# Attention scores of two heads on the two halves of the TensorE array, three products each

## The chip, the core and the metric

The kernel runs on one core of a Trainium2 chip. TensorE (PE in the profile) multiplies matrices: it loads a stationary operand of up to 128 rows and 128 columns (a weight load, PEld) and streams a moving operand through it into a bank of PSUM. VectorE (DVE), ScalarE (ACT) and GpSimd (POOL) do the elementwise work, SyncE (SP) issues the DMAs. The engines work through their own queues in order and wait for each other by semaphores. The metric is the device time of one execution in microseconds, the median of several runs.

## The reference

One layer of an encoder block on 1024 tokens of width 2048. A normalised input is projected to 5632 columns. Half of the heads do windowed softmax attention, the others a bidirectional retention; both branches are normalised and gated, mixed by an output projection, added to the input and normalised again. What matters here is the attention: 16 query heads of 64 values share 4 key/value heads, and a block of 128 queries sees its own block of keys and the two beside it.

```python
qb = q.reshape(B, nb, BLOCK, ATTN_KV_HEADS, ATTN_GROUP, ATTN_HEAD_DIM)
...
s = jnp.einsum('bnqhgd,bnkhd->bhgnqk', qb, kb).astype(jnp.float32) * scale
...
s = jnp.where(valid[None, None, None], s + bias[None], -1e30)
...
m = jnp.maximum(jnp.max(s, axis=-1, keepdims=True), sink_b)
p = jnp.exp(s - m)
p = p / (jnp.sum(p, axis=-1, keepdims=True) + jnp.exp(sink_b - m))
out = jnp.einsum('bhgnqk,bnkhd->bnqhgd', p.astype(v.dtype), vb)
```

So a pair of heads over one block of queries needs two score matrices of 128 queries by 384 keys (256 at the two ends of the sequence), with 64 terms in each sum.

## The kernel before, in words

**Precision.** Large products are made in float32r. A float32 operand is split (`split`, L103) into a high part, rounded to float32r by a copy on ACT (L104), and a low part, the difference, by a subtraction on another engine through the helper `tt` (recorded at L98). A product is then three products: high by high, high by low, low by high.

**Main products.** The input projection is a loop over 22 units of 256 columns; each unit goes through 16 slices of the contraction (k), and in each slice over four output banks (tag M) with three products a bank (L808 to L810, or L801 to L803 for units laid out token by token). Weights come in by SP's DMAs, two tiles ahead. The output projection (L890 to L892, L917 to L919) follows with the same pattern.

**Work beside them.** Attention and retention are Python generators. After each bank's products, `point()` counts one point and, if `pace` points have gone by, lets the first generator in `jobs` run to its next `yield` (`pump`). That is how one step of attention comes to stand between main products in TensorE's queue. `pace` is 4.5, 4.5, 3 and 3.8 points for the four attention groups. Nothing else sets the order of TensorE's work; the framework may move an independent instruction of another engine a little ahead in that engine's own queue.

**One attention job** (`attn_job`) is one key/value head with its four query heads. The keys are loaded twice, into rows 0 to 63 and again into rows 64 to 127, and split into `kh` and `kl`. The four query heads are two pairs (`pr`), the sequence is eight blocks (`n`); `b` counts the 16 pairs of head pair and block. Step `t` handles one head (`c`, 0 or 1) of pair `b`, so that there are 32 steps and some to finish. In step `t`:

- the scores of head `c` go into one of two score banks (`pS`, tag S): two products, L434 and L435, each of 128 rows. The rows of the query tile `q[:, c, :]` hold the high part of the 64 query values in one half and the low part in the other, and the keys stand in both halves, so that one product gives (high + low) by `kh`, the other (high + low) by `kl`: four partial products in two;
- DVE adds the bias, takes the maximum and writes the result to a tile P (L441), ACT takes the exponential (L445), and in the odd step the two heads' sums are finished and P is scaled (L453);
- in even steps from 6 on, the values of an earlier pair are multiplied (L465, L466);
- four steps after its scores, P is transposed by TensorE into the bank T (`pT`, of which there is one; L493) and split into PTh (ACT, L504) and PTl (DVE, L98).

`q_parts` makes the query tile for two blocks of a head pair: for each head a copy of 64 rows on ACT (L420) and a subtraction of 64 rows on DVE; one of the two crosses to the other half of the rows.

The prediction also uses two places outside attention: the retention's scores (`s_t`, L563, products of 64 rows) and state products (`kv`, L578, 128 rows), each written as four products and shown in the trace as eight instructions, and the column sums of `attn_norm` (L514), made on rows 0 to 63 and then on rows 64 to 127.

Of the kernel before, what the change touches and what calls it, by code (L numbers as in the profile page):

```python
# [9 lines left out]
F32 = mybir.dt.float32  # L10
F32R = mybir.dt.float32r
AF = mybir.ActivationFunctionType
ALU = mybir.AluOpType
# [19 lines left out]
def hybrid_block(ctx: ExitStack, tc: tile.TileContext, a: dict, out: bass.AP):  # L33
# [54 lines left out]
    def pS():  # L88
        return psum("S", 2)
# [7 lines left out]
    def tt(eng, o, x, y, op):  # L97
        eng.tensor_tensor(o, x, y, op)  # L98
# [29 lines left out]
                )  # L128
            A.copy(dst[:, 512 * h : 512 * h + 512], p)

# [1 line left out]
    wraw, wsp, wide = {}, {}, [None]  # L132

    def w_src(i):
# [19 lines left out]
            split(hi, lo, r, G if i < W_IN_TILES else V)  # L154
            wsp[i] = (hi, lo)

# [1 line left out]
    jobs, aux = deque(), deque()  # L158
    step = [0]
    done = set()  # L160
# [35 lines left out]
            except StopIteration:  # L196
                queue.popleft()

# [1 line left out]
    xraw = {}  # L200

    def x_load(k):
# [28 lines left out]
        yield  # L231

    def bias_rows():
        # rows of relative bias with the window's mask, repeated for the skewed read
        oh = t2()
        SP.dma_start(oh[0:33, :], a["onehot"])
        ra = small(16, "ra")
        G.memset(ra[32:33, :], 1.0)
        SP.dma_start(ra[0:32, :], a["rel_bias"])
        yield  # L240
        p = pS()
        T.matmul(p[:16, :], ra[0:33, :], oh[0:33, :], start=True, stop=True)
        bt = t2()
        V.tensor_copy(bt[:16, :], p[:16, :])
        b16 = bt[:16, :]
        SP.dma_start(bd, b16.unsqueeze(1).to_broadcast([16, 128, 512]))
        done.add("bias")
        yield
# [28 lines left out]
    def decay():  # L277
        dc = small(24, "dc")
        for dst0, name in ((0, "ret_decay_fwd"), (8, "ret_decay_bwd")):
            s = a[name]  # L280
            SP.dma_start(dc[:, dst0 : dst0 + 8], bass.AP(tensor=s.tensor, offset=s.offset, ap=[[0, 128], [1, 8]]))
            q = 16 + dst0 // 2
            for par in range(2):
                SP.dma_start(
                    dc[64 * par : 64 * par + 64, q : q + 4],
                    bass.AP(tensor=s.tensor, offset=s.offset + par, ap=[[0, 64], [2, 4]]),
                )
        jc = small(2, "jc")
        SP.dma_start(jc, a["jcol"])
        yield  # L290
        # log sigmoid: min(d, 0) - log1p(exp(-|d|)), log1p(u) = 2 atanh(u / (2 + u))
        u, z, z2, acc, lg = (small(24, n) for n in ("lu", "lz", "lz2", "lacc", "lg"))
        V.tensor_scalar(z, dc, -1.0, None, ALU.mult)
        tt(V, z, z, dc, ALU.min)
        A.activation(u, z, AF.Exp)
        V.tensor_scalar(z, u, 2.0, None, ALU.add)
        V.reciprocal(z, z)
        tt(V, z, z, u, ALU.mult)
        tt(V, z2, z, z, ALU.mult)
        yield  # L300
        V.tensor_scalar(acc, z2, 2.0 / 17, 2.0 / 15, ALU.mult, ALU.add)
        for k in (13, 11, 9, 7, 5, 3, 1):
            tt(V, acc, acc, z2, ALU.mult)
            V.tensor_scalar(acc, acc, 2.0 / k, None, ALU.add)
        tt(V, acc, acc, z, ALU.mult)
        V.tensor_scalar(lg, dc, 0.0, None, ALU.min)
        tt(V, lg, lg, acc, ALU.subtract)
        yield
        A.activation(cdec, lg[:, :16], AF.Exp, scale=128.0)
        V.tensor_scalar(kdec[:, 0:8], lg[:, 0:8], jc[:, 0:1], None, ALU.mult)  # L310
        V.tensor_scalar(kdec[:, 8:16], lg[:, 8:16], jc[:, 1:2], None, ALU.mult)
        A.activation(kdec, kdec, AF.Exp)
        V.tensor_scalar(kdec, kdec, 0.125, None, ALU.mult)
        yield
        ab = t2()
        SP.dma_start(ab, a["masks"])
        yield
        yield
        for h in range(8):
            o = t2() if h % 4 == 0 else o  # L320
            oo = o[:, 128 * (h % 4) : 128 * (h % 4) + 128]
            V.tensor_scalar(oo, ab[:, 0:128], lg[:, h : h + 1], None, ALU.mult)
            stt(V, oo, ab[:, 128:256], lg[:, 8 + h : 9 + h], oo, ALU.mult, ALU.add)
            A.activation(oo, oo, AF.Exp)
            V.tensor_scalar(oo, oo, 0.125, None, ALU.mult)
            SP.dma_start(dd[h], oo)
            yield
        for p in range(4):
            o = t2() if p % 2 == 0 else o
            oo = o[:, 256 * (p % 2) : 256 * (p % 2) + 256]  # L330
            A.activation(oo[:, 0:128], ab[:, 256:384], AF.Exp, scale=lg[:, 16 + p : 17 + p])
            A.activation(oo[:, 128:256], ab[:, 384:512], AF.Exp, scale=lg[:, 20 + p : 21 + p])
            SP.dma_start(qdd[p], oo.rearrange("p (d i) -> p d i", d=2))
            yield
        done.add("decay")

# [1 line left out]
    def k_post(tiles):  # L338
        while "rb" not in done:
            yield  # L340
# [7 lines left out]
    def gate_post(tiles, et0, key, late=None):  # L348
        for b, g in tiles:
            et, hf = b // 2, b % 2  # L350
            # 2 silu(g) = g (1 + tanh(g / 2)); the half is in ew
            e = t2()
            A.activation(e, g, AF.Tanh, scale=0.5)
            yield
            stt(V, g, e, 1.0, g, ALU.add, ALU.mult)
            c = et0 + et
            if late is None:
                SP.dma_start(gd[128 * c : 128 * c + 128, 512 * hf : 512 * hf + 512], g)
            else:
                yield  # L360
                while ("ret", 3) not in done:
                    yield
                late(et, hf, g)
            yield
        done.add(key)
# [15 lines left out]
                yield  # L381
        done.add(("rope", p))

# [1 line left out]
    acc = [None]  # L385

    def attn_job(g, q_tiles, start):
# [26 lines left out]
        def q_parts(b2):  # L414
            pr, n = divmod(2 * b2, 8)
            q = att.tile([128, 2, 256], F32R, tag="qj", name=nm("qj"), bufs=2)
            src = q_tiles[pr][:, 128 * n : 128 * n + 256]
            for c in range(2):
                s0, s1 = 64 * c, 64 * (1 - c)
                A.copy(q[s0 : s0 + 64, c, :], src[s0 : s0 + 64, :])  # L420
                tt(V, q[s1 : s1 + 64, c, :], src[s0 : s0 + 64, :], q[s0 : s0 + 64, c, :].bitcast(F32), ALU.subtract)
            qj[b2] = q

        q_parts(0)
        for t in range(32 + 8):
            if t < 32:
                b, c = divmod(t, 2)
                pr, n = divmod(b, 8)
                head = 4 * g + 2 * pr + c
                m0, m1 = max(n - 1, 0), min(n + 2, 8)  # L430
                W, k0 = 128 * (m1 - m0), 128 * (m0 - n + 1)
                q = qj[b // 2][:, c, 128 * (n % 2) : 128 * (n % 2) + 128]
                p = pS()
                T.matmul(p[:, :W], q, kh[:, 128 * m0 : 128 * m1], start=True, stop=False)  # L434
                T.matmul(p[:, :W], q, kl[:, 128 * m0 : 128 * m1], start=False, stop=True)  # L435
                if c == 0:
                    st[b] = tuple(small(2, w, 4) for w in ("nmx", "sums", "esk"))
                nmx, sums, esk = st[b]
                x = att.tile([128, 384], F32, tag="P", name=nm("P"), bufs=5)
                P[t] = x  # L440
                V.tensor_tensor_reduce(  # L441
                    x[:, :W], p[:, :W], bias[2 * pr + c][:, k0 : k0 + W], -1.0, nsink[:, head : head + 1],
                    ALU.add, ALU.min, nmx[:, c : c + 1],
                )
                A.activation(x[:, :W], x[:, :W], AF.Exp, bias=nmx[:, c : c + 1], scale=-1.0, accum_out=sums[:, c : c + 1])  # L445
                if c == 1:
                    tt(V, esk, nmx, sink[:, head - 1 : head + 1], ALU.add)
                    A.activation(esk, esk, AF.Exp)
                    tt(V, sums, sums, esk, ALU.add)
                    V.reciprocal(sums, sums)  # L450
                    for cc in range(2):
                        y = P[t - 1 + cc]
                        V.tensor_scalar(y[:, :W], y[:, :W], sums[:, cc : cc + 1], None, ALU.mult)  # L453
                if t in (4, 16):
                    load_bias(2 if t == 4 else 3)
                if t % 4 == 2 and t + 2 < 32:
                    q_parts(t // 4 + 1)
# [73 lines left out]
        done.add("attn_norm")  # L531
        yield

# [1 line left out]
    retp = [None]  # L535

    def ret_job(p, rq, rk, vt, start):
# [159 lines left out]
        yield  # L697
        done.add(("ret", p))

# [1 line left out]
    rbA = {}  # L701

    def mixed_row(pool, kk, hf, gate=None):
# [10 lines left out]
            stt(V, r, r, ew[:, kk : kk + 1], gate, ALU.mult, ALU.mult)  # L714
        split(hi, lo, r)

# [1 line left out]
    def evac(u, b, p, st):  # L718
        kind, i = UNITS[u]
        hf = b % 2  # L720
# [56 lines left out]
    for u, (kind, i) in enumerate(UNITS):  # L777
# [3 lines left out]
        for k in range(NK):  # L781
# [48 lines left out]
                mixed_row(retp[0], k - 1, 0)  # L830
            if kk == 1:
                del wsp[wi]
        # what follows from the unit
        if u == 1:
            drain(aux, "k")
        if kind == "ka":
# [236 lines left out]
```

## Time and profile before

| | |
|---|---|
| time, median of 3 runs | 1603.08 us (1602.11 to 1606.64) |
| span of the profiled execution, first to last instruction | 1599.8 us |
| TensorE busy in the span | 1539.1 us (96%) |
| weight loads busy | 1327.7 us (83%) |
| DVE, ACT, POOL busy | 800.2, 524.7, 414.2 us |
| mean granted TensorE clock | 0.987 |

The page gives no time for the profiled execution beyond its span. A busy time adds up the durations of instructions where they don't overlap; a matmul's own duration runs from its start to the end of its last result, and consecutive matmuls overlap, so what one costs the next is read from the distance of their starts. A group's row ends with the engine's idle time just before the group and what ended it.

### The profile page before, as it was taken

The page shows a single profiled execution, that of the slowest core. Times are in us where ns is not written, and L with a number is a line of the kernel's source. Part 1 is how long each engine was busy: PE and PEld are TensorE (multiplying, and loading weights), DVE is VectorE, ACT ScalarE, POOL GpSimd, SP SyncE. Part 2 cuts the span into 40 slices and gives each one's busy share as a digit, 9 for nine tenths or more (in the row PEclk, how much of TensorE's full clock was granted, in tenths as well). Part 3 has the DMA queues.
Part 4 walks back from the last instruction along what each step waited for, and adds up shares of the span by engine and source line. Part 5 has one row for each costly group of instructions (what it writes and reads, how often), then busy time and mean ns, then how long its engine had stood idle before and what let it go on. Part 6 is the DMA issues. An engine that isn't in the chain of part 4 may idle for free.

```text
span 1599.8 us, 22578 instructions
## 1 busy us (share of the span) xinstructions
PE 1539.1 (96%) x8338; PEld 1327.7 (83%) x8338; DVE 800.2 (50%) x1888; ACT 524.7 (33%) x1186; POOL 414.2 (26%) x435
## 2 busy tenths in 40 slices
PE   8947999999999999999999999999999999999997
PEld 6936888888888887888898898998998888888886
DVE  5520126662576368567624734825747563473323
ACT  5311125552455356445511111111122343433210
POOL 2201222333344334424332332323322000220000
PEclk9978999999999999999999999999999999999999
DMA  8785311331123213212231221311322465574423
GB/s 298 252 100 131 96 53 45 91 106 56 49 84 108 58 44 111 64 51 80 57 102 55 82 80 47 99 60 50 103 80 93 159 223 158 172 245 149 122 63 112
DMA packets 108442, 167.52 MB, mean 105 GB/s; under 512 B 17419, under 2 KB 38923, under 8 KB 108204
## 3 DMA queue, kind: packets, MB, share of 16 engines
q1 hardware_dynamic: 108332, 166.09, 34.9%
q8 instruction: 65, 1.06, 0.3%
q14 instruction: 45, 0.37, 0.1%
HBM read 134.06 MB, written 31.98 MB: 104 GB/s over the span
## 4 chain that ended last, share of the span: by engine, by line
PE 81%; DVE 8%; DMA 4%; issue 3%; ACT 2%; POOL 1%; SPq 0%; POOLq 0%; ACTq 0%; DVEq 0%
PE psM L808 14%; PE psM L810 13%; PE psM L809 13%; PE psM L891 4%; PE psM L890 4%; PE psM L892 4%; PE psM L802 3%; PE psM L803 3%; PE psM L801 3%; DMA wr<-in_w_in 3%; PE psT L493 2%; DVE t L101 2%; PE psS L891 1%; PE psS L890 1%; PE psS L892 1%
## 5 line engine op out<-in xcount | busy, mean ns | idle before, releaser
L808 PE MATMUL psM<-hT,wh 128*128 128x512 f32 x1088 | 442.0, 406 | 6.3 <-DVE hT L220 6.3
L810 PE MATMUL psM<-hT,wl 128*128 128x512 f32 x1088 | 425.9, 392 | 2.0 <-POOL wl L98 2.0
L809 PE MATMUL psM<-hT,wh 128*128 128x512 f32 x1088 | 425.2, 391 | 0.0
L98 POOL TENSOR_TENSOR wl<-wr,wh 128x512 fp32r<-128x512 f32 x176 | 234.2, 1331 | 602.2 <-ACT wh L104 590.5
L104 ACT CAST wh<-wr 128x512 fp32r<-128x512 f32 x288 | 178.5, 620 | 605.7 <-PE psM L809 225.6
L810 PEld LDWEIGHTS psM<-hT,wl 128*128 128x128 f32 x1088 | 204.7, 188 | 47.5 <-POOL wl L98 2.5
L808 PEld LDWEIGHTS psM<-hT,wh 128*128 128x128 f32 x1088 | 205.2, 189 | 44.4 <-issue 6.2
L809 PEld LDWEIGHTS psM<-hT,wh 128*128 128x128 f32 x1088 | 205.6, 189 | 37.3 <-DVE hT L101 0.7
L801 PE MATMUL psM<-wh,hT 128*128 128x256 f32 x640 | 184.0, 288 | 31.2 <-ACT wh L104 31.2
L802 PE MATMUL psM<-wl,hT 128*128 128x256 f32 x640 | 182.6, 285 | 2.3 <-POOL wl L98 2.3
L803 PE MATMUL psM<-wh,hT 128*128 128x256 f32 x640 | 182.2, 285 | 0.0
L801 PEld LDWEIGHTS psM<-wh,hT 128*128 128x128 f32 x640 | 124.0, 194 | 32.4 <-ACT wh L104 31.4
L98 DVE TENSOR_TENSOR wl<-wr,wh 128x512 fp32r<-128x512 f32 x112 | 84.6, 756 | 131.7 <-ACT wh L104 131.5
L802 PEld LDWEIGHTS psM<-wl,hT 128*128 128x128 f32 x640 | 124.0, 194 | 3.1 <-POOL wl L98 3.0
L803 PEld LDWEIGHTS psM<-wh,hT 128*128 128x128 f32 x640 | 123.9, 194 | 0.0
L441 DVE CUSTOM_DVE_ANT_0 P<-psS,bias,nsink 128x384 f32<-128x384 f32 (+1 forms) x128 | 74.2, 580 | 90.6 <-PE psS L435 90.2
L445 ACT ACTIVATE P<-P,nmx 128x384 f32<-128x384 f32 (+1 forms) x128 | 75.6, 590 | 94.6 <-DVE nmx L441 93.2
L890 PE MATMUL psM<-wh,hT 128*128 128x512 f32 x256 | 100.0, 390 | 0.0
L891 PE MATMUL psM<-wl,hT 128*128 128x512 f32 x256 | 99.7, 390 | 0.0
L892 PE MATMUL psM<-wh,hT 128*128 128x512 f32 x256 | 99.6, 389 | 0.0
L98 DVE TENSOR_TENSOR t<-psM,rb 128x512 f32<-128x512 f32 x64 | 42.2, 684 | 106.4 <-PE psM L810 64.9
L98 POOL TENSOR_TENSOR acc<-acc,sq 64x128 f32<-64x128 f32 x112 | 55.1, 492 | 155.8 <-ACT sq L474 145.8
(200 smaller groups left out, 2261.6 us busy)
## 6 DMA issues: line engine op xcount, KB each, us to landing
wr<-in_w_in SPq DMA_DIRECT2D x176, 256.0 KB, 2.7
wr<-in_w_out SPq DMA_DIRECT2D x112, 256.0 KB, 2.7
t<-in_x SPq DMA_DIRECT2D x16, 512.0 KB, 6.0
mr<-md SPq DMA_DIRECT2D x32, 256.0 KB, 2.9
xr<-in_x SPq DMA_DIRECT2D x32, 256.0 KB, 3.9
out<-y SPq DMA_DIRECT2D x32, 256.0 KB, 2.8
t<-in_xT SPq DMA_DIRECT2D x15, 512.0 KB, 5.1
gd<-t SPq DMA_DIRECT2D x28, 256.0 KB, 2.3
```

The costliest lines, as they stand in the source:

```text
L98: eng.tensor_tensor(o, x, y, op)
L104: A.copy(o_hi, x)
L445: A.activation(x[:, :W], x[:, :W], AF.Exp, bias=nmx[:, c : c + 1], scale=-1.0, accum_out=sums[:, c : c + 1])
L801: T.matmul(po, hh[:, sl], wh[:, ws], start=first and z == 0, stop=False, skip_group_check=True)
L802: T.matmul(po, hh[:, sl], wl[:, ws], start=False, stop=False, skip_group_check=True)
L803: T.matmul(po, hl[:, sl], wh[:, ws], start=False, stop=last, skip_group_check=True)
L808: T.matmul(p, wh[:, ws], hh[:, sl], start=first, stop=False)
L809: T.matmul(p, wh[:, ws], hl[:, sl], start=False, stop=False)
L810: T.matmul(p, wl[:, ws], hh[:, sl], start=False, stop=last)
L890: T.matmul(p, mh, wh, start=(k == 0), stop=False)
L891: T.matmul(p, mh, wl, start=False, stop=False)
L892: T.matmul(p, ml, wh, start=False, stop=(k == NK - 1))
```

## The change

`q_parts` splits both heads in place: the tile's first half-plane holds the high parts of both heads (head 0 on rows 0 to 63, head 1 on rows 64 to 127), the second their low parts, with one copy and one subtraction of 128 rows. A new function `score_pair` makes the scores of both heads of a pair in the even step, in two banks taken at once. Each head's products use only its own 64 rows of the query tile and of the keys, and there are three: high by `kh`, low by `kh`, high by `kl` (the product of the two low parts is no longer made). They are issued alternately for head 0 and head 1. The odd step issues no score products and takes the bank made before. The rest of each step is as it was; other lines of the diff only remove comments.

```diff
         def q_parts(b2):
             pr, n = divmod(2 * b2, 8)
             q = att.tile([128, 2, 256], F32R, tag="qj", name=nm("qj"), bufs=2)
-            src = q_tiles[pr][:, 128 * n : 128 * n + 256]
-            for c in range(2):
-                s0, s1 = 64 * c, 64 * (1 - c)
-                A.copy(q[s0 : s0 + 64, c, :], src[s0 : s0 + 64, :])
-                tt(V, q[s1 : s1 + 64, c, :], src[s0 : s0 + 64, :], q[s0 : s0 + 64, c, :].bitcast(F32), ALU.subtract)
+            split(q[:, 0, :], q[:, 1, :], q_tiles[pr][:, 128 * n : 128 * n + 256])
             qj[b2] = q
+
+        scores = {}
+
+        def score_pair(b):
+
+            n = b % 8
+            m0, m1 = max(n - 1, 0), min(n + 2, 8)
+            W, keys = 128 * (m1 - m0), slice(128 * m0, 128 * m1)
+            qs = slice(128 * (n % 2), 128 * (n % 2) + 128)
+            ps2 = (pS(), pS())
+            for part, kx in ((0, kh), (1, kh), (0, kl)):
+                for c in range(2):
+                    r = slice(64 * c, 64 * c + 64)
+                    T.matmul(
+                        ps2[c][:, :W], qj[b // 2][r, part, qs], kx[r, keys],
+                        start=kx is kh and part == 0, stop=kx is kl,
+                    )
+            scores[b] = ps2
...
-                q = qj[b // 2][:, c, 128 * (n % 2) : 128 * (n % 2) + 128]
-                p = pS()
-                T.matmul(p[:, :W], q, kh[:, 128 * m0 : 128 * m1], start=True, stop=False)
-                T.matmul(p[:, :W], q, kl[:, 128 * m0 : 128 * m1], start=False, stop=True)
+                if c == 0:
+                    score_pair(b)
+                p = scores[b][c]
```

## The prediction

> **What bounds the kernel now.** I began with the page's head, its busy shares and the shares of the chain that ended last.
>
> ```profile
> span 1599.8 us, 22578 instructions
> PE 1539.1 (96%) x8338; PEld 1327.7 (83%) x8338; DVE 800.2 (50%) x1888; ACT 524.7 (33%) x1186; POOL 414.2 (26%) x435
> PE 81%; DVE 8%; DMA 4%; issue 3%; ACT 2%; POOL 1%; SPq 0%; POOLq 0%; ACTq 0%; DVEq 0%
> ```
>
> TensorE sets the time: it is busy for 96% of the span and holds 81% of the chain. The change touches only the attention jobs, so I then asked for the forms of the score products (L434 and L435), whose first and last starts in the trace are at 231 and 793 us, for the busy times from 231 to 800 us, and for all that PE waited for there.
>
> ```profile
> L434 PE MATMUL psS<-t,qj 128*128 128x384 f32 x96 | 32.5, 339 | 0.0
> L435 PE MATMUL psS<-t,qj 128*128 128x384 f32 x96 | 32.3, 336 | 0.0
> L435 PE MATMUL psS<-t,qj 128*128 128x256 f32 x32 | 9.0, 281 | 0.0
> L434 PE MATMUL psS<-t,qj 128*128 128x256 f32 x32 | 9.0, 281 | 0.0
> ...
> 231.00:800.00 569.00, 562.74 (x2883) 477.71 (x2882) 343.80 (x900) 281.34 (x741) 206.72 (x258) 1.00 0.24 72
> ...
> PE psT L493 <- DVE PTl L98: 3.8, 8, 1.2
> PE psO L466 <- DVE PTl L98: 1.9, 4, 1.0
> ```
>
> The third row gives PE, PEld, DVE, ACT, POOL, then the granted clock (1.00). PE is busy 562.74 of 569.00 us while DVE has 343.80 and ACT 281.34. PE's waits there come to 3.8 + 1.9 = 5.7 us, all for the low halves of the transposed probabilities, none for a score bank (psS). So whatever TensorE needs more or less for the scores goes almost whole into the end. There are 96/2 = 48 pairs of heads with 384 keys and 32/2 = 16 with 256 at the edges of the sequence.
>
> Durations of matmuls overlap, so costs are read from starts. Columns of the following rows: start, duration, engine, line.
>
> ```profile
> 402.63 0.39 PE L810 MATMUL psM<-hT,wl 128*128 128x512 f32 x1
> 402.86 0.34 PE L434 MATMUL psS<-t,qj 128*128 128x384 f32 x1
> 403.03 0.34 PE L435 MATMUL psS<-t,qj 128*128 128x384 f32 x1
> 403.21 0.39 PE L808 MATMUL psM<-hT,wh 128*128 128x512 f32 x1
> ...
> 399.88 0.28 PE L434 MATMUL psS<-t,qj 128*128 128x256 f32 x1
> 400.00 0.28 PE L435 MATMUL psS<-t,qj 128*128 128x256 f32 x1
> 400.11 0.39 PE L808 MATMUL psM<-hT,wh 128*128 128x512 f32 x1
> ```
>
> A main product takes 402.86 - 402.63 = 0.23 us of the array, a score product 0.35 / 2 = 0.175 us with 384 keys and 0.23 / 2 = 0.115 us with 256, and nothing is lost between main products and scores.
>
> **The change, part by part.** *Score products.* Removed: four products of 128 rows a pair, 4 x 0.175 = 0.70 us, or 4 x 0.115 = 0.46 us at an edge; 48 x 0.70 + 16 x 0.46 = 41.0 us in all. Added: six products of 64 rows a pair (384 matmuls and weight loads instead of 256), alternately on the upper and the lower half of the array. If the halves work side by side, a pair takes three of them: 0.525 or 0.345 us, 48 x 0.525 + 16 x 0.345 = 30.7 us, a gain of 10.3 us. If they work one after the other it is six: 1.05 or 0.69 us, 61.4 us, a loss of 20.4 us. The trace has one place where 64-row work changes halves, the column sums of L514 (eight instructions on rows 0 to 63, then eight on rows 64 to 127), and one form with eight on one half, L563. Here are their weight loads, with the loss of array time ahead of the first in brackets.
>
> ```profile
> 820.81 1.44 PEld L514 LDWEIGHTS psS<-ones,acc 64*128 64x128 f32 x16
> ...
> 869.19 0.96 PEld L563 LDWEIGHTS psS<-t,t 64*128 64x128 f32 x8 [0.35 <-issue]
> ...
> L563 PEld LDWEIGHTS psS<-t,t x128: 182/188/188, 854.7 to 1231.9; 64*128 64x128 f32 x128
> ```
>
> One load lasts 0.188 us, so in a string on one half they follow each other every (0.96 - 0.19) / 7 = 0.11 us. Sixteen one after the other would need 15 x 0.11 + 0.19 = 1.84 us; L514's took 1.44. For about 0.4 us the two strings ran together, although they are issued string after string; the change issues them alternately. The row is of two-column products, so it shows loads and issue overlapping, not two streams of 384 keys. I take side by side and keep both ends. The second stream starts behind the first by something between 0 and one load, 0.11 us: 0 to 7.0 us over 64 pairs. I take 0.03 us, near the lower end since L514's loads overlapped, which is 1.9 us. *What a page says of that offset.* The Trainium skill, "TensorE: Matmul & The Clock Gate", section "Part 3: Packing small matmuls — row/col tiling", puts packed products on different tiles about 4 ns apart; by it the offset would be 64 x 0.004 = 0.3 us, an estimate, and the sum 1.6 us lower. No run here shows that figure so far.
>
> *Going to half the array and back.* Each pair now sits between 128-row work on both sides. The trace has the same thing with and without the half: the retention's state products (L578, 128 rows) and its scores (L563, 64 rows), both eight instructions between a main L810 and L808.
>
> ```profile
> 861.62 0.39 PE L810 MATMUL psM<-hT,wl 128*128 128x512 f32 x1
> 861.85 1.05 PE L578 MATMUL psS<-v,t 128*128 128x128 f32 x8
> 862.66 0.48 PE L808 MATMUL psM<-hT,wh 128*128 128x512 f32 x1
> 862.97 0.40 PE L809 MATMUL psM<-hT,wh 128*128 128x512 f32 x1
> ...
> 868.88 0.39 PE L810 MATMUL psM<-hT,wl 128*128 128x512 f32 x1
> 869.20 1.16 PE L563 MATMUL psS<-t,t 64*128 64x128 f32 x8
> 870.28 0.50 PE L808 MATMUL psM<-hT,wh 128*128 128x512 f32 x1
> 870.62 0.39 PE L809 MATMUL psM<-hT,wh 128*128 128x512 f32 x1
> ```
>
> From L810 to L809 it is 862.97 - 861.62 = 1.35 us with 128 rows and 870.62 - 868.88 = 1.74 us with 64: 0.39 us for the way in and out. It lies ahead of the first load (L563's bracket above): the next weights are not loaded while the last product still runs. Nothing covers it, as PE has no other work. 64 pairs x 0.39 = 25.0 us. This is the largest term; its ends are the same, as the stretch is seen with and without it.
>
> *The query split.* Removed: half of 64 copies on ACT and of 64 subtractions on DVE, each of 64 rows.
>
> ```profile
> L420 ACT CAST qj<-t x64: 389/404/408, 223.2 to 764.9; 64x256 fp32r<-64x256 f32 x64
> L98 DVE TENSOR_TENSOR qj<-t,qj x64: 418/421/1411, 223.9 to 765.8; 64x256 fp32r<-64x256 f32 x64
> ```
> ...
> L104 ACT CAST wh<-wr 128x512 fp32r<-128x512 f32 x288 | 178.5, 620 | 605.7 <-PE psM L809 225.6
> ...
> L98 DVE TENSOR_TENSOR t<-psM,rb 128x512 f32<-128x512 f32 x64 | 42.2, 684 | 106.4 <-PE psM L810 64.9
> ```
>
> The 128-row form with 256 columns isn't in the trace; it costs between the 64-row form (0.404 and 0.421 us) and the 128-row form with twice the columns (0.620 and 0.684). At the first, which has the same columns, ACT loses 32 x 0.404 = 12.9 us and DVE 32 x 0.421 = 13.5 us; at the second 6.0 and 5.1. All lies beside PE's work and can reach the end only through the 5.7 us that PE waits for DVE.
>
> *The order.* The second head's products move one step ahead: past the main products between two steps (three to four and a half points of three, 0.69 us each) and ahead of the even step's value products and transposes. No DMA moves. In the odd step the transposes lose 0.35 us of lead over DVE; in the even step DVE's first score pass comes about 0.4 us later (0.525 + 0.03 + the way in, 0.2, against 0.35), and all behind it as well; with no slack on DVE that would return as 64 x 0.4 = 26 us, but DVE is idle for 225 of the 569 us, and I take none of it. Both score banks must now be free in the even step, one of them a step after its last use instead of two.
>
> ```profile
> DVE P L441 <- PE psS L435: 90.2, 69, 3.2
> L441 DVE CUSTOM_DVE_ANT_0 P<-psS,bias,nsink x128: 470/612/619, 231.5 to 794.3; 128x384 f32<-128x384 f32 x96, 128x256 f32<-128x256 f32 x32
> ```
>
> In 69 of 128 steps DVE stood waiting for the scores, so it is seldom a step behind; a bank wait would cost at most one pass of 0.612 us a pair, 39 us, at least nothing, and I take nothing. For the 5.7 us of waits I take half as gone, because every pair gives DVE more time and four steps save it 0.42 us: -2.9 us. The ends are -5.7 and, if the odd steps' lost lead shows at each of these 12 waits, 12 x 0.35 = +4.2 us.
>
> **Sum**: 25.0 - 10.3 + 1.9 - 2.9 = +13.7 us on the profiled span of 1599.8, that is 1613.5. The median of the runs is 1603.08, 3.3 us over that span; with the same 3.3 around it the prediction is 1617 us. Side by side, the terms' own ends give 25.0 - 10.3 + 0 - 5.7 = +9.0 to 25.0 - 10.3 + 7.0 + 4.2 = +25.9 us, 1612 to 1629.
>
> **Rivals.** *One after the other.* The halves share something that L514's two-column products don't load: the six products cost +20.4 us, with 25.0 - 2.9 the change is +42.5 us and the time 1646. If only the weight loads queue, six at 0.11 us make 0.66 us for each pair: 64 x 0.66 - 41.0 = +1.2, in all +23.3 and 1626. L514's overlap speaks against both.
>
> *Faster.* The way in and out is hidden: with float32r weights, the first half loads while the other half still streams. Then -10.3 + 1.9 - 2.9 = -11.3 us, 1592. The place is the load ahead of the first score product; the point from which it decides is a way in and out of (10.3 - 1.9 + 2.9) / 64 = 0.18 us instead of 0.39. Against it stands the way back to L808 (870.28), which goes to float32r weights and is part of the 0.39.
>
> *Faster, by a rule.* If a weight load were hidden only where the next product is on other rows, the old 256 score products would each show their 0.11 us and the new ones not, a gain of up to 256 x 0.11 = 28 us on top, and the time 1589 with the ways in and out paid.
>
> ```profile
> 402.86 0.19 PEld L435 LDWEIGHTS psS<-t,qj 128*128 128x128 f32 x1
> ```
>
> But L435's load starts with L434's product at 402.86 and L435 follows 0.17 us later: it is hidden on the same rows already. The rule is the Trainium skill's, same page and section, where loads are said to overlap products "only when row_grp differs"; the trace disagrees, by that row.
>
> *No change.* The waits absorb most: with all 5.7 us gone, and as much again where PE's stream is late without a wait in the list, 25.0 - 10.3 + 0 - 11.4 = +3.3, 1606. For it: DVE holds 343.80 of 569 us in chains with ACT. Against: the list of waits is 5.7 us long.
>
> **Chances.** Slower as forecast 0.62 (1612 to 1629); one after the other or queued loads 0.14; no change 0.13; faster, either way, 0.11 (0.09 and 0.02). A measurement of this kernel tells 0.3%, 4.8 us, from no change: faster 0.11, same 0.13, slower 0.76. Range: 1602 to 1640 leaves out the faster cases and most of the fully serial one, about 0.18 together.
>
> **What would show it.** Right: the first load of each score pair starts some 0.1 us after the last product has streamed, not with it, and so does the first load behind the pair; within a pair the two heads' loads start a few tens of ns apart and each head's products follow each other every 0.175 us; the pairs together take about 0.9 us of PE from the last main product to the next, and the stretch of the scores grows from 562 us by about 14. Wrong: six products 0.175 us apart (serial), a load that starts inside the last main product (hidden way in), or a wait of PE for DVE on psS or an entry for psT well over 3.8 us (a new wait).

## The result and the profile after

The changed kernel takes 1613.87 us (median of 4 runs, 1612.99 to 1614.52) where the kernel before, run beside it, takes 1603.42: 10.45 us more, a ratio of 1.0061 with a 95% interval of 1.0047 to 1.0075. It is slower, within the range on record (1602 to 1640) and 3 us below the 1617 forecast. First the head of its page, its busy shares and the chain that ended last.

```profile
span 1612.1 us, 22866 instructions
PE 1554.3 (96%) x8466; PEld 1310.5 (81%) x8466; DVE 800.4 (50%) x1856; ACT 505.6 (31%) x1154; POOL 410.1 (25%) x435
...
PE 84%; DMA 6%; DVE 5%; issue 2%; POOL 1%; ACT 1%; SPq 0%; POOLq 0%; ACTq 0%; DVEq 0%
```

TensorE has become the chain even more (84% instead of 81%) and DVE less (5% instead of 8%). The scores are now L432, the column sums L527, the retention's scores L576. Their rows (count, shortest/median/longest ns, first and last start) beside those of the same places before, in the second fence, tell in which stretch the time was lost.

```profile
L432 PE MATMUL psS<-t,qj x384: 273/335/443, 230.6 to 796.6; 64*128 64x384 f32 x144, 64*128 64x256 f32 x48
...
L527 PE MATMUL psS<-ones,acc x16: 247/248/268, 828.6 to 829.9; 64*128 64x2 f32 x16
...
L576 PE MATMUL psS<-t,t x128: 272/272/373, 864.6 to 1243.5; 64*128 64x128 f32 x128
```

```profile
L434 PE MATMUL psS<-t,qj x128: 281/339/339, 231.1 to 792.8; 128*128 128x384 f32 x96, 128*128 128x256 f32 x32
...
L514 PE MATMUL psS<-ones,acc x16: 247/248/268, 820.8 to 822.1; 64*128 64x2 f32 x16
...
L563 PE MATMUL psS<-t,t x128: 272/272/373, 854.7 to 1232.0; 64*128 64x128 f32 x128
```

From the first score product (231.1 before, 230.6 after) to the column sums it was 820.8 - 231.1 = 589.7 us and is 828.6 - 230.6 = 598.0: 8.3 us of the loss lie in the attention jobs, where the change is. Another 2.1 us come between the column sums and the retention's first scores (33.9 before, 36.0 after); they are looked at in the last section, as is the rest of the profiled span's 12.3 us.

One score pair of the changed kernel on PE, and its weight loads (start, duration, what; brackets give the idle time ahead):

```profile
404.01 0.39 PE L822 MATMUL psM<-hT,wh 128*128 128x512 f32 x1
404.24 0.39 PE L823 MATMUL psM<-hT,wl 128*128 128x512 f32 x1
404.56 0.80 PE L432 MATMUL psS<-t,qj 64*128 64x384 f32 x6
405.29 0.50 PE L821 MATMUL psM<-hT,wh 128*128 128x512 f32 x1
405.62 0.40 PE L822 MATMUL psM<-hT,wh 128*128 128x512 f32 x1
```

```profile
404.56 0.48 PEld L432 LDWEIGHTS psS<-t,qj 64*128 64x128 f32 x6 [0.35 <-issue]
405.29 0.19 PEld L821 LDWEIGHTS psM<-hT,wh 128*128 128x128 f32 x1 [0.25 <-issue]
```

The six products sit in 0.80 us and their six loads in 0.48, so the two halves work side by side. Both ways are in the brackets: no load runs for 0.35 us ahead of the pair and 0.25 us behind it (idle time of the loads, which is more than the array time lost). From L823 to the next L822 it is 405.62 - 404.24 = 1.38 us. Two main products are 0.46 of it; 0.92 remain for the pair, and the forecast was 0.525 + 0.03 + 0.39 = 0.945.

PE's waits for other engines from 231 to 812 us, and the in-place query split (shortest/median/longest):

```profile
PE psO L479 <- DVE PTl L98: 1.4, 3, 0.5
PE psT L506 <- DVE esk L98: 0.4, 1, 0.4
```

```profile
L104 ACT CAST qj<-t x32: 401/407/408, 222.6 to 766.8; 128x256 fp32r<-128x256 f32 x32
L98 DVE TENSOR_TENSOR qj<-t,qj x32: 410/420/823, 223.2 to 767.3; 128x256 fp32r<-128x256 f32 x32
```

The waits fell from 5.7 to 1.8 us. One operation on 128 rows costs what one on 64 did (0.407 and 0.420 us), so ACT and DVE lost half of theirs.

### The profile page after: what moved, and what is told of

Read it like the earlier page. It is cut to its first block, busy times and chain, and to the rows that moved or that the text cites. A ratio compares the mean times of both kernels' runs of the same rounds, so it can differ in the third digit from the quotient of the medians.

```text
span 1612.1 us, 22866 instructions
## 1 busy us (share of the span) xinstructions
PE 1554.3 (96%) x8466; PEld 1310.5 (81%) x8466; DVE 800.4 (50%) x1856; ACT 505.6 (31%) x1154; POOL 410.1 (25%) x435
## 4 chain that ended last, share of the span: by engine, by line
PE 84%; DMA 6%; DVE 5%; issue 2%; POOL 1%; ACT 1%; SPq 0%; POOLq 0%; ACTq 0%; DVEq 0%
PE psM L821 15%; PE psM L823 15%; PE psM L822 15%; PE psM L904 4%; PE psM L903 3%; PE psM L905 3%; PE psM L815 3%; PE psM L816 3%; PE psM L814 3%; DMA wr<-in_w_in 3%; PE psS L432 3%; PE psT L506 2%; PE psO L478 2%; PE psO L479 1%; PE psS L904 1%
## 5 line engine op out<-in xcount | busy, mean ns | idle before, releaser
L821 PE MATMUL psM<-hT,wh 128*128 128x512 f32 x1088 | 444.2, 408 | 6.7 <-DVE hT L220 6.3
L823 PE MATMUL psM<-hT,wl 128*128 128x512 f32 x1088 | 426.7, 393 | 2.0 <-POOL wl L98 2.0
L822 PE MATMUL psM<-hT,wh 128*128 128x512 f32 x1088 | 425.9, 392 | 0.0
L98 POOL TENSOR_TENSOR wl<-wr,wh 128x512 fp32r<-128x512 f32 x176 | 230.3, 1309 | 606.0 <-ACT wh L104 589.2
L821 PEld LDWEIGHTS psM<-hT,wh 128*128 128x128 f32 x1088 | 205.7, 189 | 46.9 <-issue 7.8
L823 PEld LDWEIGHTS psM<-hT,wl 128*128 128x128 f32 x1088 | 204.9, 188 | 47.8 <-POOL wl L98 2.4
L822 PEld LDWEIGHTS psM<-hT,wh 128*128 128x128 f32 x1088 | 206.3, 190 | 38.0 <-DVE hT L101 0.7
```

What stands on the lines that cost most here:

```text
L821: T.matmul(p, wh[:, ws], hh[:, sl], start=first, stop=False)
L822: T.matmul(p, wh[:, ws], hl[:, sl], start=False, stop=False)
L823: T.matmul(p, wl[:, ws], hh[:, sl], start=False, stop=last)
```

## The experiments

**Are the halves really worth three products?** Both heads on one half, nothing else changed; head 1 then repeats head 0's scores and its own are left out.

```diff
-                    r = slice(64 * c, 64 * c + 64)
+                    r = slice(0, 64)
```

> The changed kernel with both heads' products on rows 0 to 63 (head 1 then computes head 0's scores; this leaves head 1 out). Same number of products, loads, banks and ways in and out, but nothing can run side by side. Theory (side by side is worth three products a pair): 48 x 0.525 + 16 x 0.345 = 30.7 us more than 1613.87, 1640 to 1645 us. Rival (the halves share a limit and the overlap in the trace's records is only of recorded starts): less than 8 us more.

Measured 1643.73 us, 29.9 above the changed kernel (ratio to the kernel before 1.026, 1.0241 to 1.0279). PE and PEld for one pair:

```profile
411.47 0.39 PE L823 MATMUL psM<-hT,wl 128*128 128x512 f32 x1
411.78 1.31 PE L432 MATMUL psS<-t,qj 64*128 64x384 f32 x6
413.03 0.50 PE L821 MATMUL psM<-hT,wh 128*128 128x512 f32 x1
```

```profile
411.78 0.99 PEld L432 LDWEIGHTS psS<-t,qj 64*128 64x128 f32 x6 [0.35 <-issue]
```

The six products take 1.31 us instead of 0.80, three more at 0.17 us each. Side by side is shown: by starts the 64 pairs together take 30.4 us more, beside the 30.7 worked out. That the whole time agrees as well is partly chance. The stretch from the first score to the column sums grew by only 27.6 us (598.0 to 625.7), as stalls went away, and 2.6 us more came between the column sums and the retention (36.0 to 38.6). The brackets and so the ways are the same.

**Does it need the alternating order?** Head by head, three and three.

```diff
-            for part, kx in ((0, kh), (1, kh), (0, kl)):
-                for c in range(2):
+            for c in range(2):
+                for part, kx in ((0, kh), (1, kh), (0, kl)):
```

> The changed kernel (1613.87 us) with the six products of a pair issued head by head, three and three, instead of alternately. Theory (the halves start whatever lies within reach of TensorE's queue, as the second string of the column sums L514 did when four of its first string's eight were under way): the second head still starts beside the first, 1612 to 1620 us. Rival (products start strictly in the order of the program, so the second head comes only when the first one's third product has started, two products of 0.175 us later): 48 x 0.35 + 16 x 0.23 = 20.5 us more, about 1634 us.

Measured 1613.53 us (1.0066, 1.0046 to 1.0087), the changed kernel's time.

```profile
406.86 0.39 PE L823 MATMUL psM<-hT,wl 128*128 128x512 f32 x1
407.18 0.80 PE L432 MATMUL psS<-t,qj 64*128 64x384 f32 x6
407.91 0.50 PE L821 MATMUL psM<-hT,wh 128*128 128x512 f32 x1
```

Still six in 0.80 us, though in TensorE's queue the second head's first product now stands behind the first head's third. The rival of a strict order falls.

**The price of the ways by itself.** The kernel before with one more product a pair ahead of the even step's scores, into the bank that the next product starts afresh: on 64, on 128, on 96 and on 32 rows (the number in the two slices).

```diff
                 p = pS()
+                if c == 0:
+                    T.matmul(p[:, :W], q[0:64, :], kh[0:64, 128 * m0 : 128 * m1], start=True, stop=True)
```

> The kernel before (1603.42 us) with one more product a pair ahead of the even step's scores, of 64 rows, into the bank that the next product starts afresh. Theory (0.39 us for each way onto half the array and back): 64 x 0.39 = 25.0 us and the product itself 48 x 0.175 + 16 x 0.115 = 10.2 us, less up to 7 us of waits that a slower TensorE absorbs: 1632 to 1639 us. Rival (no price of its own where float32r products follow each other): 1607 to 1614 us.

> The same added product with 128 rows instead of 64. Theory: only its 10.2 us, less up to 7 us of absorbed waits: 1607 to 1614 us, and 25 us (22 to 26) below the version with 64 rows. Rival (an added product costs the same whatever its rows): both the same.

> The kernel before with the added product a pair on 96 rows instead of 64 or 128. If the price belongs to working on half the array, 96 rows need the whole and cost only the product: 1607 to 1614 us as with 128 rows. If it belongs to any change of the number of rows: about 1628 us as with 64.

> The same added product on 32 rows. If each way costs the drain of what streams before it, whatever part of the array follows: about 1628 us as with 64 rows. If a quarter of the array costs more to reach than a half: above 1632 us.

Measured: 64 rows 1628.32 us (1.0161, 1.0146 to 1.0176), 128 rows 1610.80 (1.0052, 1.0036 to 1.0069), 96 rows 1612.71 (1.0057, 1.0038 to 1.0075), 32 rows 1629.11 (1.0165, 1.0144 to 1.0186). So 96 rows cost what 128 do and 32 what 64 do: the price belongs to leaving the whole array, not to a changed number of rows. The places show it, first 64 rows, then 96.

```profile
402.05 0.39 PE L812 MATMUL psM<-hT,wl 128*128 128x512 f32 x1
402.37 0.38 PE L435 MATMUL psS<-t,qj 64*128 64x256 f32 x1
402.68 0.39 PE L436 MATMUL psS<-t,qj 128*128 128x256 f32 x1
402.90 0.28 PE L437 MATMUL psS<-t,qj 128*128 128x256 f32 x1
```

```profile
405.54 0.39 PE L812 MATMUL psM<-hT,wl 128*128 128x512 f32 x1
405.77 0.34 PE L435 MATMUL psS<-t,qj 96*128 96x384 f32 x1
405.95 0.34 PE L436 MATMUL psS<-t,qj 128*128 128x384 f32 x1
406.12 0.33 PE L437 MATMUL psS<-t,qj 128*128 128x384 f32 x1
```

From L812 to L437 it is 402.90 - 402.05 = 0.85 us with 64 rows, of which 0.23 + 2 x 0.115 = 0.46 are the products: 0.39 us for the ways, as expected. With 96 rows it is 0.58 = 0.23 + 2 x 0.175: nothing.

But the times differ by only 17.5 us (64 against 128 rows), not by the 22 to 26 expected, and 1628.32 us lies under the 1632 to 1639 expected for 64 rows. PE's waits in the attention stretch, first with 64 rows, then with 128, tell where some of the rest went:

```profile
PE psT L495 <- DVE PTl L98: 0.6, 2, 0.4
```

```profile
PE psT L495 <- DVE PTl L98: 3.0, 8, 0.8
PE psO L468 <- DVE PTl L98: 1.3, 2, 0.9
```

4.3 us of waits became 0.6. The list counts only the part of a stall that is left after the last result of the product before. Taken from the starts of all matmuls from the first score to the column sums instead (places where the next one came over 60 ns later than the median for the same neighbours, ways left out), the stalls are 9.8 us in the kernel before, 7.6 with 128 rows and 2.0 with 64: 25.0 - 5.6 = 19.4, which is what this stretch differs by in the two profiled executions (597.4 and 616.8 us). A slower TensorE pays for itself in part because DVE is then less late.

**Twice as many ways.** The changed kernel's products and tiles, each head in its own step.

```diff
-                if c == 0:
-                    score_pair(b)
-                p = scores[b][c]
+                p = score_head(b, c)
```

(`score_head` is `score_pair` for the one head `c`, with one bank.)

> The changed kernel's products and query tiles, but each head's three products in its own step as before: 128 ways onto half the array and back instead of 64, and nothing beside each string. Theory: 64 x 0.39 = 25.0 us more for the ways and 30.7 us for three products a pair that no longer run side by side, less a few us of waits: 1613.87 + 55.7 - 4 = 1663 to 1670 us. Rival (the price of a way is a wait hidden in the pair's issue, paid once a pair): about 1645 us.

Measured 1662.13 us (1.0365, 1.0346 to 1.0385), 48.3 above the changed kernel. That is 1 us under the range expected and 17 above the rival's 1645. One head of an edge block here, and, in the second fence, one edge pair of the changed kernel:

```profile
302.65 0.39 PE L817 MATMUL psM<-hT,wl 128*128 128x512 f32 x1
302.97 0.62 PE L428 MATMUL psS<-t,qj 64*128 64x256 f32 x3
303.51 0.38 PE L472 MATMUL psO<-PTh,t 128*128 128x256 f32 x1
```

```profile
397.68 0.62 PE L432 MATMUL psS<-t,qj 64*128 64x256 f32 x6
```

Three products of one head take the 0.62 us that six of two heads take side by side. PE no longer waits for any engine in this kernel's attention stretch. The sum against the kernel before is 2 x 25.0 + 20.4 (six products instead of four) less its stalls, 9.8 us by starts: +60.6; measured 1662.13 - 1602.74 = +59.4. The attention stretch itself grew by 57.3 us (589.7 to 647.0): by starts a visit to half the array costs 0.34 us instead of 0.39 where a transpose follows. Some 2 us of the measured difference lie outside the stretch, so the nearness of the two totals is partly chance.

**What took the waits away?** Three runs on the kernel before. First the order: both heads in the even step, four products of 128 rows.

```diff
-                q = qj[b // 2][:, c, 128 * (n % 2) : 128 * (n % 2) + 128]
-                p = pS()
-                T.matmul(p[:, :W], q, kh[:, 128 * m0 : 128 * m1], start=True, stop=False)
-                T.matmul(p[:, :W], q, kl[:, 128 * m0 : 128 * m1], start=False, stop=True)
+                if c == 0:
+                    pair = (pS(), pS())
+                    for z in range(2):
+                        q = qj[b // 2][:, z, 128 * (n % 2) : 128 * (n % 2) + 128]
+                        T.matmul(pair[z][:, :W], q, kh[:, 128 * m0 : 128 * m1], start=True, stop=False)
+                        T.matmul(pair[z][:, :W], q, kl[:, 128 * m0 : 128 * m1], start=False, stop=True)
+                p = pair[c]
```

> The kernel before with one part of the change alone: both heads' scores in the even step, still four products of 128 rows and the old query tiles. It tells why TensorE's waits for DVE shrank in the changed kernel. If the order does it (the odd step's score pass no longer waits for TensorE): 2 to 6 us below 1603.42, 1597 to 1601 us. If it is TensorE's own slower pace, or the split in place: 1602 to 1605 us. If the lost lead of 0.35 us in the odd step counts: up to 1608 us.

Measured 1604.30 us beside 1602.74 (1.0007, 0.9997 to 1.0016): no change that can be told. Then the split in place alone, with the old products on its tiles (each score mixes two heads):

```diff
-            src = q_tiles[pr][:, 128 * n : 128 * n + 256]
-            for c in range(2):
...
+            split(q[:, 0, :], q[:, 1, :], q_tiles[pr][:, 128 * n : 128 * n + 256])
```

> The kernel before with the queries split in place (one copy and one subtraction of 128 rows for two heads) and the old products of 128 rows on these tiles; each score then mixes the two heads, so this computes something else in the same number of products. If the 26 us that ACT and DVE no longer spend are what took TensorE's waits away: 2 to 6 us below 1603.42, 1597 to 1601 us. If they lie beside TensorE's work: 1602 to 1605 us.

Measured 1598.66 us (0.9969, 0.9959 to 0.9980): 4.1 us faster. PE's waits of the attention stretch, first for the order alone, then for the split alone:

```profile
PE psO L469 <- DVE PTl L98: 3.4, 4, 1.0
PE psT L496 <- DVE esk L98: 1.7, 4, 0.7
```

```profile
PE psT L489 <- DVE PTl L98: 2.7, 5, 1.5
PE psO L462 <- DVE PTl L98: 0.3, 1, 0.3
```

The order mostly moves the waits: 5.1 us instead of 5.7, now most on the value products (psO) instead of the transposes (psT). The split halves them, to 3.0. Last, DVE's share alone: the 64 subtractions on POOL, the scores as they were.

```diff
-                tt(V, q[s1 : s1 + 64, c, :], src[s0 : s0 + 64, :], q[s0 : s0 + 64, c, :].bitcast(F32), ALU.subtract)
+                tt(G, q[s1 : s1 + 64, c, :], src[s0 : s0 + 64, :], q[s0 : s0 + 64, c, :].bitcast(F32), ALU.subtract)
```

> The kernel before with the 64 subtractions of the query split on POOL instead of DVE, scores as they were. DVE loses 64 x 0.421 = 27 us of the attention stretch, ACT nothing. If DVE's share is what the split in place (1598.66 us beside 1602.74) won: 1597 to 1601 us. If ACT's copies were the part that counted: 1601 to 1605 us. If POOL's longer operation (1.33 us for 512 columns, so about 0.7 us for 256) holds up the weights' low halves behind it: above 1605 us.

Measured 1601.14 us beside 1603.36 (0.9990, 0.9979 to 1.0001), on the line between the first two cases and not told from no change. The profiled executions, one each, say a little more: the attention stretch took 589.7 us before, 587.9 with the order alone, 584.1 with the split alone and 586.6 with the subtractions on POOL, with stalls by starts of 9.8, 8.2, 4.7 and 7.0 us. There DVE's share is about half of the split's, but how much of the split's 4.1 us is ACT's copies and how much DVE's subtractions stays open. The split in place does not fit products of 128 rows, which want each head's high and low part in the same columns, so with these tiles its gain was not to be had without the halves; no version here that computes all scores beats the kernel before by more than the measurement can tell.

## Why the prediction was right

**The ways in and out, 25.0 us.** Right. From the starts of the changed kernel's matmuls the 64 visits cost 25.0 us in all; 0.39 us is found again in the added product of 64 rows, and not with 96 or 128. Only where it lies was half right. The prediction put it all ahead of the first load; by starts 0.09 us passes there on each way, and about 0.1 us more is that load itself, which nothing hides: L822 comes 0.33 us after L821 instead of 0.23, and a half's second product 0.28 us after its first instead of 0.175. It was the one large term, and it was in the trace of before, in two neighbouring places that differ only in their rows.

**Side by side, -10.3 us.** Right: making it impossible cost 30.4 us by starts, of the 30.7 worked out. The rival of one after the other falls with it, and so does that of queued loads: six loads in 0.48 us, where six at 0.11 us would need 5 x 0.11 + 0.19 = 0.74.

**The offset, +1.9 us.** Too high. In the starts of single products (the views above merge the six), the second head's stands 3 ns behind the first head's (404.560 and 404.563 us in the pair shown; the median of all is the same): 64 x 0.003 = 0.2 us in all. The 4 ns that the Trainium skill gives ("TensorE: Matmul & The Clock Gate", "Part 3: Packing small matmuls — row/col tiling") agrees with these starts far better than the prediction's 0.03.

**The waits, -2.9 us.** The mis-sized term. By starts, stalls in the attention stretch fell from 9.8 us to 3.8: -6.0 us. The prediction read 5.7 us from the list of waits, which leaves out the first part of each stall, and took half. Two causes are shown, and they do not add: the split in place alone brings the time down by 4.1 us, and a slower TensorE alone lets 5.6 us of stalls go (64 against 128 rows). The new bank wait was rightly taken at nothing: no wait of PE on psS is listed.

**The sum.** With these sizes it is 25.0 - 10.3 + 0.2 - 6.0 = +8.9 us; the attention stretch grew by 8.3. The forecast's +13.7 was 3.3 us over the measured +10.45. Its errors in offset and waits come to 1.7 + 3.1 = 4.8 us, and 2.1 us between the column sums and the retention, which it did not have, made up for part of them: that it came so near is in part luck.

**The rivals that it would be faster** fall by the brackets ahead of the pair: no load starts while the last main product streams. The rule that loads are hidden only across rows falls once more, in the run on one half: its six products follow each other as fast as products of 128 rows did, 0.17 us, loads hidden on the same rows. "No change" had the right mechanism, waits that absorb, at about half of its size (6.0 us instead of 11.4).

## What to carry to other kernels

Leaving the whole array and coming back costs 0.39 us here (0.34 where a transpose follows), however little is done there, so half-array work pays only when a visit saves more than that: three products of 384 columns instead of four save 0.175 us, and the visit must hold more than twice as much. Price it from a place that already does it in the trace, beside a neighbour that does not, and check first whether the whole-array form wastes much: here it did four partial products in two. Where TensorE is the bound, a stall is counted from the distance of starts, and a part of what is added to TensorE comes back as stalls that vanish.

## What the runs showed beyond this

**Order.** In the run head by head, the second head's products ran beside the first head's although they were issued after them (by single starts 10 ns behind, instead of 3): the queue's order, which the beginning of this document gives for every engine, does not hold on TensorE between the two halves. The Trainium skill, "TensorE: Matmul & The Clock Gate", section "The mechanism" of Part 3, has matmuls in strict order of start and end; six products in 0.80 us in that run disagree with it for the starts.

**Rows.** A product of 96 rows goes as one of 128 and pays no way in or out; one of 32 rows pays what one of 64 does.

**A short pause and the clock.** Between column sums and retention, PE waits 2.0 us for POOL in both kernels. In the changed kernel's profiled execution the granted clock then fell, and the main products came every 0.43 us instead of 0.23 for a while. PE's timeline there, and the busy times (PE, PEld, DVE, ACT, POOL, then the clock) of 8 us around it:

```profile
856.76 0.80 PE L823 MATMUL psM<-hT,wl 128*128 128x512 f32 x1 [2.01 <-POOL wl L98]
857.35 0.63 PE L821 MATMUL psM<-hT,wh 128*128 128x512 f32 x1
857.78 0.63 PE L822 MATMUL psM<-hT,wh 128*128 128x512 f32 x1
```

```profile
852.00:860.00 8.00, 5.65 (x25) 4.37 (x24) 2.68 (x5) 2.19 (x5) 5.85 (x3) 0.79 0.31 84
```

The same stretch of the kernel before, around the same wait, kept its clock:

```profile
844.00:852.00 8.00, 5.98 (x34) 4.95 (x34) 2.29 (x5) 2.19 (x5) 5.49 (x3) 1.00 0.28 84
```

8 x (1 - 0.79) = 1.7 us are lost, most of the 2.1. The changed kernel's profiled execution has a second dip in the retention, which took 378.9 us from its first to its last score product instead of 377.3:

```profile
1212.00:1224.00 12.00, 10.37 (x48) 8.47 (x49) 6.44 (x19) 4.15 (x7) 2.31 (x2) 0.86 0.47 152
```

Here 12 x (1 - 0.86) = 1.7 us are lost. The profiled executions head by head, with both heads on one half (there after a wait of 4.4 us), with the order alone, with the split alone and with the subtractions on POOL had the first dip as well; those with 32 to 128 rows added and the one with each head in its own step did not, though PE waited there for 1.9 to 2.1 us too, and the one with 96 rows had the second dip. So such a pause alone does not bring it about, and what decides stays open; each is a single execution.

The mean granted clock of the other runs tells something of its share in the 10.45 us. Of 44 runs of the kernel before, 18 had a clock of 0.988 and took 1601.87 us in the median; 17 had 0.985 or 0.986 and took 1604.96. The four runs of the changed kernel had 0.985 to 0.987. The one run with 0.988 of its head-by-head form took 1610.13 us, 8.3 more than 1601.87 and as much as the attention stretch grew. By that one run some 8 us are the change's own and 2 such dips', an estimate.
